# All 31 convolution taps on VectorE, a new order of a half, and the plan's durations taken from traces

## The chip, the cores and the metric

The kernel runs on 1 core of one Trainium2 chip. The metric is the device time of one execution in microseconds; lower is better. Before the change it is 1961.19 us, the median of 3 runs (1960.9 to 1964.42).

## The reference, cut to what matters

One layer of a hybrid decoder on 2048 prompt tokens and 8 single-token samples, width 1024, all in float32:

```
h    = rmsnorm(x)
proj = h @ w_in            # 48 chunks of 128 columns: c_a 8, c_b 8, c_z 8, s_x 4, s_z 4, g_c 8, g_s 8
u    = c_a * sigmoid(c_b)
v    = causal depthwise conv of u, 31 taps per channel, + bias
y_c  = (silu(layernorm(v)) * silu(c_z)) @ w_pc
y_s  = grouped complex-diagonal SSM of s_x, gelu, * sigmoid(. @ w_glu), * silu(s_z), @ w_ps
m    = sigmoid(g_c) * y_c + sigmoid(g_s) * y_s
x1   = x + rmsnorm(m @ w_out)
y    = x1 + rmsnorm(p @ w_ple) * sigmoid(x1 @ w_pg)
```

The outputs are y for both groups of tokens, the convolution's last inputs, and the SSM's states.

## The kernel before, in words

Channels lie on the 128 partitions, tokens along the free axis. The tokens are worked in two halves: half 0 is 1024 prompt tokens and the 8 samples (blocks of 344 columns, 258 for w_out and w_pg), half 1 the other 1024 (blocks of 512). Every float32 product is three passes over split operands: `hi` is a rounding to the fast matmul type, `lo` the rest, and each product sums hi·hi, hi·lo and lo·hi (`stages`, lines 289 to 291). A weight chunk of 512 KB is loaded from the SP queue, its `hi` cast on ScalarE, its `lo` subtracted on GpSimd (`w_split`), and `w_ahead` requests chunks two to three stages ahead in the fixed list `order`.

`half` runs the stages of a half on TensorE in this order: SX (SSM input, 4 chunks; in half 0 first for the first block, then for the other two), then CB and CA of each of 8 channel tiles, which give `u`; GC (8 chunks, stored to DRAM); SZ; w_glu; then GS two chunks at a time with w_ps; CZ (8 chunks); w_pc; w_out; w_pg. w_pc sums over all 8 tiles of `v`, so it can't begin until the layer norm has gone through all of them.

All else is laid beside these stages by a planner written out in Python (`Background`): tasks are generators that name an engine and a ready time; `pump` lets them emit instructions up to the planned time `bg.pe` of TensorE, by priority; `drain` emits a task's rest. Engines take instructions in the order emitted, so a wrong planned duration leaves a wrong order behind. The durations are `cV` (VectorE), `cS` (ScalarE), `cG` (GpSimd) and, per matmul, n/2400 + 0.003 us. A task that yields "P" puts small matmuls into TensorE's stream.

The tasks that matter here:

- `ssm_setup` (priority 6): small operations on VectorE for the SSM's parameters, then phases e^(i·k·theta) by doubling (`unit_length`, `cmul`: chains on 8 channels times 1, 2, 4 ... 64 elements), then four tables: VectorE makes `gt` from `gw`, TensorE transposes it (line 610) and multiplies it (620), GpSimd makes `cq`.
- `ssm_batch` (four a half): loads, matmuls (720), rotation by the phases and a scan on VectorE, matmuls (775, 778), and loads back.
- `conv_task` (priority 10): for each tile an opening multiplication and 30 multiply-adds of 1024 elements on VectorE, the sum `acc` in PSUM. If 8 units of SBUF are free, `conv_side` takes taps from the other end: ScalarE scales half a tile (`cq`, line 882), GpSimd adds it to `ca`; VectorE then adds `ca` (tile `u<-acc,ca`).
- `ln_task` (priority 4): sum over tiles, the mean by a matmul with a constant matrix, then per tile subtraction and square, a norm, and per tile scale, Silu, product with CZ's output and split into `vh`, `vl`.

SBUF is handed out in 38 units of 128 x 1096 elements; `room(k)` holds a task until k are free.

Of the kernel before, what the change touches and what calls it, by code (L numbers as in the profile page):

```python
# [13 lines left out]
P = 128  # L14
# [9 lines left out]
NUNIT = 38  # L24
UW = 1096


class Background:
# [105 lines left out]
def build(nc, tc, A, O):  # L134
# [23 lines left out]
    with ExitStack() as ctx:  # L158
# [60 lines left out]
        for h in range(2):  # L219
            if h == 0:  # L220
                order += [("w_ple", j) for j in range(2)]
            for _ in range(2 if h == 0 else 1):
                order += [("w_in", SX + b) for b in range(4)]
            for c in range(8):
                order += [("w_in", CB + c), ("w_in", CA + c)]
            order += [("w_in", GC + c) for c in range(8)]
            order += [("w_in", SZ + b) for b in range(4)]
            order += [("w_glu", j) for j in range(2)]
            for j in range(4):
                order += [("w_in", GS + 2 * j), ("w_in", GS + 2 * j + 1), ("w_ps", j)]  # L230
# [51 lines left out]
        def stages(key, todo):  # L282
            wt, k = take(key)
            for i, (m, rhs, evac, c0, n) in enumerate(todo):
# [9 lines left out]
                bg.pe += 3 * k * (n / 2400.0 + 0.003)  # L294
# [3 lines left out]
        def stage_pair(keys, rhs, blocks, evacs):  # L298
# [12 lines left out]
            bg.pe += 6 * len(rhs) * sum(n / 2400.0 + 0.003 for _, n in blocks)  # L311
# [36 lines left out]
        def mean_task(acc, blocks, bias, ready, k, split):  # L348
# [11 lines left out]
            yield "P", ready  # L360
# [32 lines left out]
        def norm_task(acc, blocks, ready, split=False):  # L393

            c = slice(blocks[0][0], blocks[-1][0] + blocks[-1][1])
            (tmp, y), r = yield from mean_task(acc, blocks, epsc, ready, 2, split)
# [14 lines left out]
        ud_d = [dram.tile([P, HT + NS], F32, name=f"ud{b}") for b in range(NB)]  # L411
        yd_d = [dram.tile([P, 8, 136], F32, name=f"yd{b}") for b in range(NB)]
# [18 lines left out]
        MAGIC = 12582912.0  # L431

# [15 lines left out]
        tables = {"done": 0}  # L448

        def ssm_setup():  # L450
# [20 lines left out]
            r0 = use("V", 5.6, 3.0)  # L471
# [8 lines left out]
            r0 = use("V", 1.6, r0)  # L480
# [25 lines left out]
            r0 = use("V", 4.0, r0)  # L506
# [19 lines left out]
            r0 = use("V", 6.0, r0)  # L526
# [16 lines left out]

            yield "V", r0
            tt(k1, mag, mag)
            tt(k1, k1, k1)
            tt(rho, k1, k1)
            ph = [[k1, k2], [k3, nre]]

            def unit_length(re, im, t):  # L550

                tt(t[0], re, re)
                tt(t[1], im, im)
                tt(t[0], t[0], t[1], ALU.add)
                ts(t[0], t[0], -0.5, 1.5)
                tt(re, re, t[0])
                tt(im, im, t[0])

            v2 = [wk[:, x * 16:x * 16 + 16] for x in range(2)]
            V.tensor_copy(out=ph[0][0], in_=cs)  # L560
            V.tensor_copy(out=ph[0][1], in_=sn)
            for x in range(3):
                unit_length(*ph[0], v2)
                cmul(*ph[1], *ph[0], *ph[0], *v2)
                ph.reverse()
            r0 = use("V", 6.5, r0)
            for x in range(2):
                yield from room(3)
                pu2 = [alloc(name="ph") for _ in range(3)]
                un = [t[:, 0:1024].rearrange("p (j k) -> p j k", k=P) for t in pu2[0:2]]  # L570
                w2 = [pu2[2][:, y * 512:(y + 1) * 512].rearrange("p (j k) -> p j k", j=8) for y in range(2)]
                s2 = [t[:, 0:8] for t in v2]
                yield "V", r0
                for r in range(2):
                    V.tensor_copy(out=un[r][:, :, 0], in_=ph[0][r][:, x * 8:x * 8 + 8])
                m = 1
                while m < P:
                    unit_length(un[0][:, :, m - 1], un[1][:, :, m - 1], s2)
                    base = [u_[:, :, m - 1:m].to_broadcast([P, 8, m]) for u_ in un]
                    cmul(un[0][:, :, m:2 * m], un[1][:, :, m:2 * m], un[0][:, :, 0:m], un[1][:, :, 0:m],  # L580
                         *base, w2[0][:, :, 0:m], w2[1][:, :, 0:m])
                    m *= 2
                    r0 = use("V", 2.0 + 6 * cV(4 * m), r0)
                    yield "V", r0
                for b in range(2 * x, 2 * x + 2):
                    for r in range(2):
                        dma(out=ph_d[b][:, r * 512:(r + 1) * 512],
                            in_=pu2[r][:, (b - 2 * x) * 512:(b - 2 * x + 1) * 512], after=r0)
                free(*pu2)
            r1 = max(r0, r1)  # L590
            for b in range(NB):
# [11 lines left out]
                r1 = use("V", 6 * cV(512), r1)  # L603
                we = alloc(name="we")
                wev = we[:, 0:1024].rearrange("p (j i r s) -> p j i r s", i=2, r=2, s=64)
                for r in range(2):
                    yield "P", r1
# [7 lines left out]
                yield "P", r1  # L615
# [7 lines left out]
                free(gt)  # L623
                yield "V", r3
# [13 lines left out]
                free(kdu, we)  # L638
                cq = alloc(name="cq")
# [18 lines left out]
                tables[b] = queue["data"] + 1.0  # L658
            free(bb, bcu, cbd, pu)
# [16 lines left out]
        def ssm_batch(h, b, sx, ysb, n, ready):  # L676
# [25 lines left out]
            phu = alloc(name="sph")  # L702
            rp = dma(out=phu[:, 0:1024], in_=ph_d[b], after=tables[b])
# [8 lines left out]
            for j0 in range(0, 4, 2):  # L712
                yield "P", r
# [16 lines left out]
            r = max(r1, rp)  # L730
# [16 lines left out]
            r = use("V", 2 * cV(1024) + 2 * cV(512), r)  # L747
# [6 lines left out]
            r = use("V", 8 * cV(256), r)  # L754
# [3 lines left out]
            r = use("V", 2 * cV(1024) + 2 * cV(512) + 0.2, r)  # L758
# [9 lines left out]
            for j0 in range(0, 4, 2):  # L768
                yield "P", r
# [51 lines left out]
        def conv_task(h, us, vs, seen):  # L821
            for c in range(NT):
                while us[c] is None:
                    yield None, bg.now + 0.5
# [9 lines left out]
                use("V", 0.4)  # L834
# [10 lines left out]
                use("V", 1.33)  # L845
                while left["lo"] <= left["hi"]:
# [6 lines left out]
                    r = use("V", 1.33)  # L853
# [34 lines left out]
        def sample_conv_task(seen):  # L888

            w = lambda c, k: cw[:, c, k:k + 1]  # L890
            for c in range(NT):
# [12 lines left out]
                use("V", 1.0, r)  # L904
# [23 lines left out]
        def embed(wait):  # L928

            for j in range(2):  # L930
                def ev_of(h, j=j):
# [3 lines left out]
                    def ev(m, o, c0, nn):  # L935
# [3 lines left out]
                        if c0 == 344:  # L939
                            V.tensor_copy(out=ts_[m][:, c0:c0 + nn], in_=o)  # L940
                            fore("V", cV(nn) + 0.06)
# [24 lines left out]
        def rms_task(todo):  # L966

            for nm, h in todo:
# [25 lines left out]
                r = yield from norm_task(acc, BLOCKS[h], ra, True)  # L994
# [85 lines left out]
        def half(h, hT, finish):  # L1080
# [16 lines left out]
            for k, part in enumerate(PARTS[h] if h == 0 else [[0, 1]]):  # L1097
                if finish:
                    finish(k)
                def ev_of(b):  # L1100
# [21 lines left out]
            us, vs = [None] * NT, [None] * NT  # L1122
            seen = [0, 0]
# [100 lines left out]
            def ln_sub(c, mean, acc, r):  # L1224
# [3 lines left out]
                if c:  # L1228
                    yield from room(1)
# [357 lines left out]
```

## Time and profile before

| what | value |
|---|---|
| runs | 1960.9, 1961.19, 1964.42 us; median 1961.19 |
| the profiled execution, in all | 1960.78 us |
| its span, first to last instruction | 1959.0 us |
| mean granted TensorE clock | 0.991 |
| busy share TensorE, VectorE, ScalarE, GpSimd | 98%, 73%, 39%, 40% |
| DMA | 243.63 MB, mean 124 GB/s |

The profile is one execution. "Busy" of TensorE joins overlapping matmuls, whose ends are modelled; a matmul's mean duration is therefore longer than the spacing between two of them. The granted clock is a share of full speed. Times in timelines count from the span's start.

### The profile page before, as it was taken

The page shows a single profiled execution, that of the slowest core. Times are in us where ns is not written, and L with a number is a line of the kernel's source. Part 1 is how long each engine was busy: PE and PEld are TensorE (multiplying, and loading weights), DVE is VectorE, ACT ScalarE, POOL GpSimd, SP SyncE. Part 2 cuts the span into 40 slices and gives each one's busy share as a digit, 9 for nine tenths or more (in the row PEclk, how much of TensorE's full clock was granted, in tenths as well). Part 3 has the DMA queues.
Part 4 walks back from the last instruction along what each step waited for, and adds up shares of the span by engine and source line. Part 5 has one row for each costly group of instructions (what it writes and reads, how often), then busy time and mean ns, then how long its engine had stood idle before and what let it go on. Part 6 is the DMA issues. An engine that isn't in the chain of part 4 may idle for free.

```text
span 1959.0 us, 27432 instructions
## 1 busy us (share of the span) xinstructions
PE 1915.9 (98%) x10772; PEld 1723.5 (88%) x10772; DVE 1438.4 (73%) x1703; ACT 769.3 (39%) x1301; POOL 784.2 (40%) x573
## 2 busy tenths in 40 slices
PE   8897999999999999999999999999999999999998
PEld 7897999999999999999997888888788888888876
DVE  6889997899899876446674579888499843341786
ACT  7424211228311364255533223455731353223542
POOL 1437523315422233234452222786743223224554
PEclk9898999999999999999999999999999999999999
DMA  8461334542122215334564563222112311432455
GB/s 316 152 209 56 106 133 142 181 141 71 57 89 80 99 43 194 120 95 144 193 207 162 183 204 119 65 65 97 66 43 76 99 65 44 161 108 86 140 193 172
DMA packets 103290, 243.63 MB, mean 124 GB/s; under 512 B 11752, under 2 KB 41576, under 8 KB 103144
## 3 DMA queue, kind: packets, MB, share of 16 engines
q1 hardware_dynamic: 102840, 241.68, 37.0%
q8 instruction: 84, 1.38, 0.3%
q14 instruction: 46, 0.38, 0.1%
q10 hardware_dynamic: 320, 0.20, 0.0%
HBM read 188.17 MB, written 54.62 MB: 124 GB/s over the span
## 4 chain that ended last, share of the span: by engine, by line
PE 84%; DVE 4%; issue 3%; POOL 2%; ACT 2%; DMA 1%; SPq 0%; ACTq 0%; POOLq 0%; DVEq 0%
PE bank L289 27%; PE bank L291 26%; PE bank L290 26%; PE bank L775 2%; POOL ca L332 1%; PE bank L778 1%; PE bank L720 1%; DVE sgp L332 1%; POOL wlo L332 1%; DVE o L183 1%; DMA raw<-in_w 1%; DVE spar L183 0%; DVE o L332 0%; PE bank L620 0%; DMA xn<-in_xT 0%
## 5 line engine op out<-in xcount | busy, mean ns | idle before, releaser
L332 POOL TENSOR_TENSOR wlo<-raw,whi 128x512 fp32r<-128x512 f32 x386 | 565.7, 1484 | 1072.2 <-ACT whi L252 1056.8
L289 PE MATMUL bank<-hh,whi 128*128 128x344 f32 (+1 forms) x1888 | 666.1, 353 | 0.9 <-ACT whi L252 0.9
L290 PE MATMUL bank<-hl,whi 128*128 128x344 f32 (+1 forms) x1888 | 661.4, 350 | 5.3 <-DVE hl L332 5.3
L291 PE MATMUL bank<-hh,wlo 128*128 128x344 f32 (+1 forms) x1888 | 659.8, 349 | 1.5 <-POOL wlo L332 1.5
L183 DVE SCALAR_TENSOR_TENSOR acc<-u,prm,acc 128x1024 f32<-128x1024 f32 x412 | 530.5, 1288 | 11.2
L289 PEld LDWEIGHTS bank<-hh,whi 128*128 128x128 f32 x1888 | 356.6, 189 | 37.5 <-ACT whi L252 1.5
L290 PEld LDWEIGHTS bank<-hl,whi 128*128 128x128 f32 x1888 | 357.1, 189 | 36.8 <-DVE hl L332 5.6
L291 PEld LDWEIGHTS bank<-hh,wlo 128*128 128x128 f32 x1888 | 357.4, 189 | 34.7 <-POOL wlo L332 2.5
L252 ACT CAST whi<-raw 128x512 fp32r<-128x512 f32 x388 | 223.9, 619 | 144.0 <-PE bank L290 68.7
L289 PE MATMUL bank<-mh,whi 128*128 128x258 f32 (+1 forms) x768 | 247.0, 322 | 2.2 <-ACT mh L339 1.7
L291 PE MATMUL bank<-mh,wlo 128*128 128x258 f32 (+1 forms) x768 | 246.6, 321 | 1.7 <-POOL wlo L332 1.6
L290 PE MATMUL bank<-ml,whi 128*128 128x258 f32 (+1 forms) x768 | 246.5, 321 | 0.4 <-DVE ml L332 0.3
L291 PEld LDWEIGHTS bank<-mh,wlo 128*128 128x128 f32 x768 | 145.6, 190 | 14.3 <-POOL wlo L332 3.0
L289 PEld LDWEIGHTS bank<-mh,whi 128*128 128x128 f32 x768 | 145.4, 189 | 14.2 <-ACT mh L339 1.9
L290 PEld LDWEIGHTS bank<-ml,whi 128*128 128x128 f32 x768 | 145.5, 189 | 12.5 <-DVE ml L332 1.0
L332 POOL TENSOR_TENSOR ca<-ca,cq 128x512 f32<-128x512 f32 x104 | 132.3, 1300 | 38.9 <-ACT cq L882 35.6
L290 PE MATMUL bank<-vl,whi 128*128 128x344 f32 (+1 forms) x320 | 111.9, 350 | 0.7 <-DVE vl L332 0.7
L289 PE MATMUL bank<-vh,whi 128*128 128x344 f32 (+1 forms) x320 | 112.0, 350 | 0.0
L291 PE MATMUL bank<-vh,wlo 128*128 128x344 f32 (+1 forms) x320 | 111.9, 350 | 0.0
L882 ACT ACTIVATE cq<-u,prm 128x512 f32<-128x512 f32 x104 | 73.4, 722 | 55.1 <-POOL ca L332 46.0
L332 DVE TENSOR_TENSOR oacc<-oacc,sq 128x258 f32<-128x258 f32 (+1 forms) x42 | 29.7, 721 | 70.2 <-ACT sq L1389 69.9
L177 DVE TENSOR_TENSOR gcl<-bank,gcl 128x344 f32<-128x344 f32 (+1 forms) x40 | 23.5, 587 | 65.4 <-PE bank L291 65.3
(213 smaller groups left out, 2452.0 us busy)
## 6 DMA issues: line engine op xcount, KB each, us to landing
raw<-in_w SPq DMA_DIRECT2D x194, 512.0 KB
cq<-cq SPq DMA_DIRECT2D x12, 512.0 KB
e<-e SPq DMA_DIRECT2D x8, 516.0 KB
rt<-e SPq DMA_DIRECT2D x8, 516.0 KB
gc<-gc SPq DMA_DIRECT2D x8, 516.0 KB
m<-gs SPq DMA_DIRECT2D x8, 516.0 KB
gcl<-gc SPq DMA_DIRECT2D x8, 516.0 KB
m2l<-m SPq DMA_DIRECT2D x8, 516.0 KB
```

Source lines behind the costliest of these rows:

```text
L177: V.tensor_tensor(out=out, in0=a, in1=b, op=op)
L183: V.scalar_tensor_tensor(out=out, in0=a, scalar=s, in1=b, op0=op0, op1=op1)
L252: S.copy(out=hi, in_=t[:, c])
L289: T.matmul(o, hi[:, w], rh[:, c0:c0 + n], start=kt == 0, stop=False)
L290: T.matmul(o, hi[:, w], rl[:, c0:c0 + n], start=False, stop=False)
L291: T.matmul(o, lo[:, w], rh[:, c0:c0 + n], start=False, stop=kt == k - 1)
L332: (V if e == "V" else GP).tensor_tensor(out=out, in0=a, in1=b, op=op)
L720: T.matmul(pvs[rr][half_[i], jj], we[:, g * P + rr * 64:g * P + rr * 64 + 64], U[:, g, 8:8 + ne], start=True, stop=True)
L775: T.matmul(pvs[i][:, jj], TW[:, :, 2 * j + i], U[:, 2 * j + i, o0:136], start=True, stop=False)
L778: T.matmul(pvs[i][:, jj], cq[half_[i], x * 512 + j * P:x * 512 + (j + 1) * P], X[half_[i], x, j, o0:136], start=False, stop=x == 1)
L882: S.activation(out=q[:, h], in_=u[:, k + x * 512:k + x * 512 + 512], func=AF.Identity, scale=w(k))
```

## The change

1. **Order of a half.** In half 0, CB and CA of two tiles (`EARLY`) come first, for the first block and then for the other two, in SX's place; SX follows once, for all blocks. Each later pair CB, CA (in half 1 each of the eight) is followed by two of the 16 gate chunks (GC, then GS); both gates go to DRAM. The rest of the gates come after, then SZ, w_glu, w_ps (its gates loaded back by `load_gs`), CZ, w_pc, w_out, w_pg.
2. **Taps.** `conv_side` is not started any more: all 31 taps on VectorE.
3. **Spilling.** After a tile of `v` is in the layer norm's sum, tiles 0 to 5 (`NSPILL`) are stored to `v_d` in DRAM. `back_task` is added when w_ps's stages are emitted, and loads them again; the norm's subtraction waits for it.
4. **Phases.** Instead of the doubling chains: angle times 1 to 128 on GpSimd, range reduction on VectorE, sine and cosine on ScalarE, double angle and length correction on GpSimd and VectorE, for 1024 elements at a time, in a task of its own (priority 6.1) that the tables don't wait for.
5. **Plan.** New durations; small matmuls of the SSM, the tables and most norms yield "Q", which is "P" with 9 us (`MARGIN`) added to the ready time; more `room` waits.

```
-        return "V" if v + n / 960.0 <= g + n / 478.0 + 0.3 else "G"
+        return "V" if v + n / 760.0 <= g + n / 440.0 + 0.4 else "G"
-    cV = lambda n: 0.08 + n / 960.0
+    cV = lambda n: 0.12 + n / 760.0
+    cVp = lambda n: 0.13 + n / 950.0
-    cS = lambda n: 0.13 + n / 1250.0
-    cG = lambda n: 0.16 + n / 478.0
+    cS = lambda n: 0.15 + n / 1100.0
+    cG = lambda n: 0.3 + n / 440.0
+    cPr = lambda n: 0.007 + n * 0.4375e-3
...
+                if e == "Q":
+                    e, r = "P", r + MARGIN
...
-            r0 = use("V", 5.6, 3.0)
+            r0 = use("V", 11.0, 3.0)
...
+            def phases(x, r):
...
+                r = ew("G", v3(a), kb, part(hi), ALU.mult, 1024, r)
+                r2 = ew("G", v3(cp), kb, part(lo), ALU.mult, 1024, r)
+                yield "V", r
+                ts(q, a, MAGIC, None, ALU.add)
+                stt(a, q, -MAGIC, a, ALU.add, ALU.subtract)
...
+                S.activation(out=sp, in_=a, func=AF.Sin, scale=PI)
+                S.activation(out=cp, in_=q, func=AF.Sin, scale=-PI, bias=hpi)
...
-                yield "P", r
+                yield "Q", r
...
-                if units.left() >= 8:
-                    left["hi"] -= 1
-                    a2 = alloc(name="ca")
-                    side = bg.add(conv_side(c, u, a2, left, bg.clock["V"] + 0.2), 9.5)
...
+                    if c < NSPILL and not lnt["back"]:
+                        yield None, r
+                        dma(out=v_d[h][c * P:(c + 1) * P, 0:n], in_=v, after=r)
+                        free(vs[c][0])
...
+            def back_task():
+                lnt["back"] = True
+                for c in list(lnt["out"]):
+                    yield from room(6)
+                    t = alloc(name="v")
+                    vs[c] = t, dma(out=t[:, PAD:PAD + n], in_=v_d[h][c * P:(c + 1) * P, 0:n])
...
+            for c in range(0 if h else EARLY, NT):
+                u_tile(c, blocks)
+                for _ in range(2):
+                    gate(gate_at)
+                    gate_at += 1
...
+            bg.add(back_task(), 3.8)
```

## Rows read from the trace of the kernel before

**Rows 1.** The page's first part: busy us, share, instructions of each engine.
```profile
PE 1915.9 (98%) x10772; PEld 1723.5 (88%) x10772; DVE 1438.4 (73%) x1703; ACT 769.3 (39%) x1301; POOL 784.2 (40%) x573
```

**Rows 2.** TensorE's waits, whole span: releaser, us in total, times, longest.
```profile
PE bank L610 <- issue: 14.1, 1, 14.1
...
PE bank L290 <- DVE hl L332: 5.3, 1, 5.3
```

**Rows 3.** Windows: length, busy us (instructions) of each engine, granted clock, DMA share, GB/s.
```profile
49.00:98.00 49.00, 41.96 (x224) 39.51 (x224) 42.55 (x101) 23.37 (x41) 21.74 (x30) 0.90 0.44 152
...
1029.00:1078.00 49.00, 45.79 (x214) 37.09 (x213) 23.69 (x22) 15.36 (x24) 13.87 (x10) 0.97 0.49 161
...
1470.00:1519.00 49.00, 49.00 (x214) 39.72 (x213) 45.97 (x40) 8.91 (x16) 16.47 (x12) 1.00 0.24 77
```

**Rows 4.** Timeline of TensorE at line 610: start, us, line, tiles, [idle before].
```profile
181.70 0.32 PE L290 MATMUL bank<-hl,whi 128*128 128x344 f32 x1
181.86 0.32 PE L291 MATMUL bank<-hh,wlo 128*128 128x344 f32 x1
196.23 1.09 PE L610 MATMUL bank<-ident,gt 128*128 128x128 f32 x4 [14.06 <-issue]
...
197.40 0.49 PE L290 MATMUL bank<-hl,whi 128*128 128x344 f32 x1
197.69 0.49 PE L291 MATMUL bank<-hh,wlo 128*128 128x344 f32 x1
```

**Rows 5.** Windows of 10 us at the stop, columns as in rows 3.
```profile
190.00:200.00 10.00, 3.77 (x15) 3.80 (x16) 9.69 (x18) 1.21 (x2) 1.28 (x1) 0.50 0.45 159
200.00:210.00 10.00, 10.00 (x67) 9.98 (x67) 9.75 (x10) 4.77 (x8) 5.25 (x5) 0.93 0.13 52
```

**Rows 6.** Timeline of VectorE ahead of the stop.
```profile
174.65 1.15 DVE L177 TENSOR_TENSOR spar<-spar 128x8 f32<-128x8 f32 x1
...
188.23 0.17 DVE L177 TENSOR_TENSOR spar<-spar 128x8 f32<-128x8 f32 x1
...
195.44 0.69 DVE L177 TENSOR_TENSOR gt<-gw 128x512 f32<-128x512 f32 x1
```

**Rows 7.** Timeline of GpSimd in the same stretch.
```profile
174.44 7.94 POOL L332 TENSOR_TENSOR ca<-ca,cq 128x512 f32<-128x512 f32 x6
```

**Rows 8.** Groups by line and form: busy us, mean ns, idle time before.
```profile
L183 DVE SCALAR_TENSOR_TENSOR acc<-u,prm,acc 128x1024 f32<-128x1024 f32 x412 | 530.5, 1288 | 11.2
...
L332 POOL TENSOR_TENSOR ca<-ca,cq 128x512 f32<-128x512 f32 x104 | 132.3, 1300 | 38.9 <-ACT cq L882 35.6 <-PE bank L291 3.4
...
L177 DVE TENSOR_TENSOR u<-acc,ca 128x1024 f32<-128x1024 f32 x6 | 7.3, 1224 | 31.9 <-POOL ca L332 31.8
```

**Rows 9.** Windows of tile ca alone: VectorE, ScalarE, GpSimd, then clock, DMA.
```profile
0.00:1040.00 1040.00, 1.22 (x1) 1.23 (x1) 33.49 (x26) 0.99 0.41 136
1040.00:1960.00 920.00, 6.12 (x5) 6.21 (x5) 98.79 (x78) 1.00 0.34 111
```

**Rows 10.** Window of tile ph alone: VectorE.
```profile
98.00:196.00 98.00, 55.85 (x144) 0.94 0.42 133
```

**Rows 11.** Windows up to the last tap of each half, columns as in rows 3.
```profile
98.00:667.00 569.00, 554.54 (x3602) 546.53 (x3601) 519.63 (x710) 174.30 (x320) 211.47 (x167) 0.99 0.35 115
1098.00:1534.00 436.00, 435.69 (x2030) 353.79 (x2029) 369.29 (x346) 180.43 (x275) 226.12 (x160) 1.00 0.30 98
```

**Rows 12.** Timeline of VectorE: the layer norm's stretch in both halves.
```profile
679.30 1.23 DVE L332 TENSOR_TENSOR u<-u,mean 128x1032 f32<-128x1032 f32 x1 [3.32 <-ACT mean L375]
...
754.46 1.23 DVE L332 TENSOR_TENSOR vl<-cz,vh 128x1032 fp32r<-128x1032 f32 x1 [1.12 <-ACT vh L339]
...
1543.21 1.23 DVE L332 TENSOR_TENSOR u<-u,mean 128x1024 f32<-128x1024 f32 x1 [5.52 <-ACT mean L375]
...
1594.27 5.10 DVE L332 TENSOR_TENSOR u<-u,acc 128x1024 f32<-128x1024 f32 x3
```

**Rows 13.** Tile vh: w_pc's weight loads, ns min/median/max, first and last start.
```profile
L289 PEld LDWEIGHTS bank<-vh,whi x320: 187/188/193, 751.3 to 1770.4; 128*128 128x128 f32 x160
```

More of the change, by code (lines that the diff above doesn't have):

```diff
@@ L24 @@
 NUNIT = 38
+NSPILL = 6
+MARGIN = 9.0
+EARLY = 2
 UW = 1096
@@ L310, in stage_pair @@
             w_ahead(wstate["use"], 0)
-            bg.pe += 6 * len(rhs) * sum(n / 2400.0 + 0.003 for _, n in blocks)
+            bg.pe += 6 * len(rhs) * sum(cPr(n) for _, n in blocks)
             bg.pump(pe=False)
@@ L346, in hilo, with mean_task @@
             return alloc(F32R, name=name + "h"), alloc(F32R, name=name + "l")
-        def mean_task(acc, blocks, bias, ready, k, split):
+        def mean_task(acc, blocks, bias, ready, k, split, late=False):
             yield from room(3 if split else k)
@@ L411, in build @@
         ud_d = [dram.tile([P, HT + NS], F32, name=f"ud{b}") for b in range(NB)]
+        v_d = [dram.tile([D, HT + NS], F32, name=f"v{h}") for h in range(2)]
         yd_d = [dram.tile([P, 8, 136], F32, name=f"yd{b}") for b in range(NB)]
@@ L446, in exp_dve @@
             tt(out, q, ki.bitcast(F32))
-        tables = {"done": 0}
+        tables = {"done": 0, "phases": 0}
         def ssm_setup():
@@ L505, in ssm_setup @@
             tt(fim, k1, k3)
-            r0 = use("V", 4.0, r0)
+            r0 = use("V", 7.0, r0)
+            yield "V", r0
+            tt(rho, mag, mag)
+            tt(rho, rho, rho)
+            tt(rho, rho, rho)
+            kk = pu[:, 944:1072]
+            yield "G", 0.0
+            GP.memset(kk[:, 0:1], 1.0)
+            m = 1
+            while m < P:
+                GP.tensor_scalar(out=kk[:, m:2 * m], in0=kk[:, 0:m], scalar1=float(m), scalar2=None, op0=ALU.add)
+                m *= 2
@@ L507, in ssm_setup, with phase_task @@
+            def phase_task(r):
+                for x in range(2):
+                    yield from phases(x, r)
+            bg.add(phase_task(r0), 6.1)
             yield "V", r0
@@ L658, in ssm_setup @@
                 tables[b] = queue["data"] + 1.0
+            while tables["phases"] < NB:
+                yield None, bg.now + 0.5
             free(bb, bcu, cbd, pu)
@@ L729, in ssm_batch @@
             free(we)
-            r = max(r1, rp)
+            while tables["phases"] < b + 1:
+                yield None, bg.now + 1.0
+            yield from room(3)
+            phu = alloc(name="sph")
+            r = max(r1, dma(out=phu[:, 0:1024], in_=ph_d[b], after=tables["ph", b // 2]))
+            yield from room(2)
             tmp, tm2 = alloc(name="stmp"), alloc(name="stmq")
@@ new lines, in half, with ln_sub @@
+            cz, vT = [None] * NT, [None] * NT
+            zr = [0.0] * NT
+            lnt = {"back": False, "out": []}
+            def back_task():
[4 more added lines that the diff above has]
+                    vs[c] = t, dma(out=t[:, PAD:PAD + n], in_=v_d[h][c * P:(c + 1) * P, 0:n])
+            def ln_sub(c, mean, acc, r):
+                r = max(r, vs[c][1])
+                yield "V", r
+                v = vs[c][0][:, PAD:PAD + n]
+                r = ew("V", v, v, mean[:, full], ALU.subtract, n, r)
+                if c:
+                    yield from room(1)
+                q = alloc(name="sq") if c else acc
+                yield "S", r
+                S.activation(out=q[:, full], in_=v, func=AF.Square)
+                r = use("S", cS(n), r)
+                if c:
+                    while not lnt["sub"][0][3]:
+                        yield None, bg.now + 0.5
+                    e = bg.pick(n, r)
+                    yield e, r
+                    r = ew(e, acc[:, full], acc[:, full], q[:, full], ALU.add, n, r)
+                    free(q)
+                lnt["r"] = max(lnt["r"], r)
@@ L1099, in half @@
+            ln = bg.add(ln_task(), 4)
+            conv = bg.add(conv_task(h, us, vs, seen), 10)
+            samp = bg.add(sample_conv_task(seen), 9) if h == 0 else None
+            if h == 0:
+                for k, part in enumerate(PARTS[h]):
                     finish(k)
+                    for c in range(EARLY):
+                        u_tile(c, [blocks[i] for i in part])
+            for part in [list(range(len(blocks)))]:
                 def ev_of(b):
@@ L1294, in half, with load_gs @@
-            ln = bg.add(ln_task(), 4)
+            gl = {}
+            def load_gs(j):
+                gl[j] = [unit("gs") for _ in range(2)]
+                for m, t in enumerate(gl[j]):
+                    dma(out=t[:, 0:n], in_=m2_d[h][(2 * j + m) * P:(2 * j + m + 1) * P, 0:n])
+            load_gs(0)
             for j in range(4):
-                gs = [unit("gs") for _ in range(2)]
-                for x in range(2):
-                    stage(("w_in", GS + 2 * j + x), hT, blocks, act_to(gs[x], AF.Sigmoid))
```

345 lines of the change are left out of this document (179 added, 166 removed).

## The prediction

> **What bounds the kernel now.** I read the page's first part first: TensorE is busy 1915.9 of 1959 us, every other engine at most 73% [rows 1]. So the end is set by TensorE's own stream, and a change that issues the same matmuls can only win what TensorE loses, or add to it. The steady rate shows that the matmuls themselves can't shrink: 344 columns start every 0.16 us [rows 4], 512 columns every 49.00/214 = 0.229 us [rows 3]. The idle time is 1959.0 - 1915.9 = 43.1 us. The waits of TensorE name one stop above all, 14.1 us at line 610; the next that the change touches is 5.3 us for `hl` of the first half [rows 2]. The windows put some loss in the first 98 us and around the change of halves, with the clock at 0.90 and 0.97 there [rows 3].
>
> The stop at line 610 is the transpose of `gt`, a table of the SSM that the plan placed in TensorE's stream among the matmuls of the big stages. TensorE reached it at 182.2 us; VectorE finished `gt` at about 196.1 [rows 4, 6]. The reason is on VectorE: the chain of phases ahead of `gt` works on 8 elements at a time, and such an instruction takes 0.17 us while GpSimd is quiet (at 188.23) but 1.15 us while GpSimd adds taps to `ca` (at 174.65; six of them run from 174.44 to 182.38) [rows 6, 7]. The plan priced neither.
>
> **The change part by part.** TensorE's work is the same: as many weight tiles, blocks and small SSM matmuls as before, in another order. What moves is what it waits for.
>
> 1. *The stop at line 610 goes.* The phase chain leaves VectorE (55.85 us of it between 98 and 196 us, counting only what touches `ph` [rows 10]), `gt` no longer stands behind it, GpSimd adds no taps, and the SSM's TensorE pieces are placed 9 us later than the planner thinks them ready ("Q"). Worth 14.06 us of idle time, and the slow restart: the granted clock is 0.50 from 190 to 200 us and 0.93 from 200 to 210 [rows 5], and matmuls of 344 columns start every 0.29 us instead of 0.16 at first [rows 4]. That is the lower of the two levels, 1.2 GHz, until about 200 + 0.07 x 10 x 2 = 201.4 us; from 196.2 to 201.4 half of 5.2 us is lost, 2.6. Together 16.7 us. Bounds: 0, if the stop only moves, and 16.7. I take 16.7, since cause and cover are both addressed. What is late next at this place is the same `gt` behind GpSimd: six table operations planned at 6 x (0.12 + 512/760) = 4.8 us. The new phases put 14 operations of 1024 elements on GpSimd, each about 2 x 1.3 = 2.6 us by the adds of 512 [rows 8]; if each of the six waits out one, they take 15.6 us, 10.8 over the plan, 1.8 more than the margin.
>
> 2. *All taps on VectorE.* GpSimd made 26 half-width adds in half 0 and 78 in half 1, which is 13 and 39 taps, with 1 and 5 opening taps on ScalarE and as many joining adds on VectorE [rows 9]. Half 0: VectorE gains 14 x 1.288 - 1.22 = 16.8 us; half 1: 44 x 1.288 - 6.1 = 50.6 us [rows 8]. Against it half 0 loses the 55.85 us, and gets eight phase operations of at most 1.288 us, 10.3. None of this is on TensorE's path as long as the layer norm's inputs are ready when CZ begins (point 4). GpSimd loses 132.3 us and gets 14 x 2.6 = 36; its other work is the weight split, which leaves it 60% idle [rows 1], so I cost both at nothing.
>
> 3. *Is the convolution in time?* Half 0: from 98 us to the end of the last tap at 667 VectorE was busy 519.6 of 569 us, 91% [rows 11]. Now 519.6 + 16.8 - 55.85 + 10.3 = 490.9 us; at 91% this takes 538 us and ends at 636 (at 100% at 589). CZ takes 8 x 72 x 0.157 = 90.4 us ahead of w_pc, which began at 751.3 [rows 13], so it began at 660.9 and now, 16.7 earlier, at 644. Half 1: 369.3 + 50.6 = 420 us from 1098 - 17 = 1081; 31.9 us of VectorE's idle time were waits for `ca` that go [rows 8], so its share is 369.3/404 = 91% and the end 1081 + 461 = 1542. CZ of half 1 begins at 1770.4 - 88.1 (the last weight load of w_pc less 8 x 48 x 0.229) - 88.1 - 16.7 = 1577.
>
> 4. *Layer norm now starts when CZ does, and must end with it.* Six of eight convolved tiles go out to DRAM and come back after w_ps. The loads are 0.52 MB each, 3.2 us at the 161 GB/s of the busiest row shown [rows 3]; VectorE takes about 2.5 us a tile, so all but the first 3 to 5 us lie beside the subtraction of the mean. The stretch from the first subtraction to the last `vl` was 679.3 to 755.7 = 76.4 us in half 0 [rows 12]. With 4 us of load and 9 us of margin ahead of the variance's matmul this is 89.4 us, against 90.4 of CZ. In half 1 subtraction to last scaling took 1543.2 to 1599.4 = 56.2 us; with eight products and splits of 2 x 1.23 us behind it 75.9, plus 13 = 88.9 against 88.1. So both just fit. The mean's own 15 us (split, margin, matmul) lie before CZ in half 1, and in half 0 end at 651, 7 us into CZ: there 76.4 + 9 from 651 ends at 736, w_pc is due at 751.3 - 16.7 = 734.6. Cost of this point: 0 to 5 us, I take 1, as the 76.4 contain 4 us of waits for CZ itself.
>
> 5. *The new waits.* The SP queue gets 8 more gate stores, 8 gate loads and 12 stores and loads of `v_d` a half. A store of `v_d` waits for the norm's sum, and behind it in that queue stand the next weight loads; w_ahead requests them two to three stages ahead, 22 to 34 us at 72 x 0.157 = 11.3 us a stage, so a store late by less costs nothing. The 28 x 0.52 = 14.5 MB a half more is some 90 us of transfer at 161 GB/s [rows 3], spread over 600 us: hidden.
>
> 6. *The start.* CB and CA of two tiles take SX's place, same matmuls. VectorE gets 6 evacuations of 344 elements, each below the 1.288 us of 1024 [rows 8], in the stretch where TensorE waited 5.3 us for `hl` [rows 2]. Bounds: 7.7 us lost, or up to 10.2 won (5.3, and 0.10 x 49 of clock [rows 3]) if the honest price of the SSM setup now keeps it from getting ahead of the last `hl`. I take 0.
>
> Sum: the profiled execution took 1960.8 us in all (span 1959.0), 0.4 below the median of 1961.2, so I work from it: 1960.8 - 16.7 + 1 = **1945 us**, by the first case's own uncertainty 1937 to 1952.
>
> **The rivals.**
>
> *A. The honest prices also win back the start and the change of halves.* Start 5.3 + 4.9; from 1029 to 1078 us 3.2 of idle time and 0.03 x 49 = 1.5 of clock [rows 3]. 1945 - 15 = 1930. For: those waits, too, stand behind VectorE work that the old plan priced low (`cV` for 1024 elements says 1.15 us, the subtractions took 1.23 or more [rows 12]). Against: no edit is aimed at them.
>
> *B. VectorE becomes the bound ahead of w_pc, and the kernel slower.* Every microsecond by which the last tap of half 0 passes 636 goes through the norm into a stop before w_pc. If VectorE runs at 86% (waits for the more closely planned evacuations, GpSimd's blocking), the taps end at 98 + 571 = 669, 33 us past 636, of which 1 to 3 are in the sum already: 1945 + 30 = 1975. It decides from 490.9/554 = 89% on: there the taps end at 652 and the gain of 16 is used up. For: the norm fills CZ to the microsecond in both halves. Against: in the stretch before, VectorE lost its time to waits that the new plan places later. The Trainium skill (Perfetto Trace Analysis, section "Optimizing Scalar/DVE Operations") would speak for B: work of a saturated VectorE is better moved to ScalarE or even GpSimd, though it adds that VectorE and GpSimd share a read port, so that the move may not help. That the old taps on GpSimd slowed VectorE nearly sevenfold on small operations (0.17 to 1.15 us) is the part that this trace shows.
>
> *C. The stop stays in another form.* `gt` waits behind the phase work on GpSimd (point 1: 10.8 us late against 9 of margin, on each of up to four tables): 1.8 us at each of four tables, 7, or, if the tables also queue behind the rest of the phases, up to most of the old stop: 1947 to 1960, say 1955. For: 0.17 against 1.15 us beside GpSimd [rows 6, 7]. Against: the table operations need not meet the phases at all. The Trainium skill (SBUF — State Buffer, section "Who interferes with whom") states it as a rule: a VectorE instruction with two SBUF inputs and a GpSimd instruction that reads SBUF block each other, whichever comes second for the whole of the first. By that rule this move of phases to GpSimd has its price on VectorE; the small operations of this trace agree with it, and what 1024-element operations do to a table operation no row here shows.
>
> **How the numbers follow.** A difference under 0.2% (3.9 us) can't be told from none. Forecast 1945: 0.50. A: 0.17. B: 0.20. C: 0.13, half of it within 0.2%. So faster 0.50 + 0.17 + 0.07 = 0.74, same 0.06, slower 0.20. For 8 in 10 the range goes to A with a little below, and into the first half of B: 1926 to 1970.
>
> **What would show it.** Right: TensorE's waits name line 610 no more, and the clock is full from 180 to 210 us; GpSimd's `ca` group is gone; VectorE has some 480 tap instructions of 1.29 us; the last `vl` falls within about 3 us of the first matmul of w_pc in both halves. B would show as a wait of TensorE for `vh` or `vl`, with VectorE at taps after 650 us. C as waits at the lines of the transposes or at 720 to 780 in the old numbering. A as no wait for `hl` and full clock from 60 to 90 us. I am wrong if a new wait above 5 us stands at a place not named here, most likely on a weight load behind a store.

## The result, and the profile after

The changed kernel takes 2011.22 us, the median of 4 runs (2009.71 to 2012.44), beside 1961.05 us for the kernel before on the same chip (4 runs, 1960.41 to 1964.42): ratio 1.0252, 95% interval 1.0234 to 1.027. It is 50 us slower, where 1945 was forecast and 1970 was the top of the range. The profiled span is 2007.9 us.

First the busy time of each engine in the kernel after; it answers [rows 1].

```profile
PE 1935.0 (96%) x10772; PEld 1732.8 (86%) x10772; DVE 1439.9 (72%) x1565; ACT 712.5 (35%) x1208; POOL 683.4 (34%) x491
```

TensorE has the same 10772 matmuls. VectorE is no busier than before (1439.9 against 1438.4 us). No other engine became the bound; TensorE lost time. Its waits in the kernel after, answering [rows 2]:

```profile
PE bank L300 <- ACT whi L263: 22.3, 5, 6.9
PE bank L300 <- ACT mh L350: 10.5, 2, 10.3
PE bank L302 <- POOL wlo L343: 6.8, 6, 3.6
PE bank L300 <- ACT vh L350: 4.5, 2, 4.2
...
PE bank L300 <- ACT ynh L350: 3.3, 2, 1.7
PE bank L301 <- DVE ynl L343: 3.1, 3, 2.0
```

The stop at the transpose is gone from this list, and the windows at its place are full (answer to [rows 5]):

```profile
190.00:200.00 10.00, 10.00 (x82) 8.98 (x80) 9.79 (x9) 9.76 (x15) 6.91 (x5) 1.00 0.18 52
200.00:210.00 10.00, 10.00 (x69) 10.00 (x69) 9.71 (x12) 2.85 (x9) 5.21 (x5) 1.00 0.67 214
```

In its place stand waits for `whi` and `mh` (the stages w_out and w_pg), `wlo` (the last weight chunk of SZ above all), `ynh` and `ynl` (w_ps) and `vh` (w_pc). The longest wait for `whi`, 6.9 us, is no new one: it stands ahead of the very first matmul, as in the kernel before, so 15.4 of the 22.3 us lie elsewhere. From the waits of the kernel before:

```profile
PE bank L289 <- ACT whi L252: 8.3, 3, 6.9
```

The windows show where TensorE lost its time:

```profile
560.00:620.00 60.00, 52.28 (x304) 50.18 (x303) 51.86 (x56) 22.10 (x37) 24.32 (x13) 0.94 0.30 99
740.00:780.00 40.00, 33.41 (x196) 31.96 (x195) 25.32 (x30) 16.98 (x23) 7.25 (x5) 0.91 0.43 146
900.00:940.00 40.00, 32.74 (x252) 32.17 (x251) 24.32 (x35) 20.17 (x44) 14.09 (x10) 0.87 0.39 128
...
1940.00:1960.00 20.00, 9.10 (x35) 6.29 (x34) 12.17 (x16) 5.00 (x9) 7.01 (x4) 0.74 0.59 195
```

The last column but two is the granted clock, 0.74 to 0.94 here, and a list of waits leaves out what the lower clock after each stop costs. So I also took, from TensorE's timeline, each gap from one large matmul's start to the next start, less the steady gap (0.157 us for 344 columns, 0.230 for 512, 0.1205 for 258) and less the small matmuls between, and summed the excess by stage. This table, in us, is my working from the timelines of the kernels named in it. Its totals differ by 50.4 us between before and after, the spans by 48.9. The column w_ps takes in the SZ stages just ahead: of the 18.4 us, 11.0 are waits for w_ps's own input and 7.4 waits of SZ for its weights' split.

```
                           start  SSM tables   w_ps   ahead of   w_out,  change of   rest  total
                           <105   and scan            w_pc       w_pg    halves
before                     15.3    20.1         0.0     1.0        8.3      6.4       2.1   53.2
after                      15.5     2.8        18.4     9.5       43.5     11.5       2.4  103.6
e1 old scaling price       14.9     2.8        19.2     9.6       15.9      2.2       2.3   66.8
e2 all old durations       10.9     9.0        19.4    34.5        9.1      5.9       2.0   90.9
e3 gates late              14.8     3.9         0       9.6       41.6     11.4       2.3   83.5
e4 before + new durations  16.1    25.2         0       1.0       44.3     11.5       9.4  107.5
e5 before + scaling price  15.4    20.1         0.0     1.0       45.4      2.3       2.5   86.7
e6 = e1 and e3             15.4     3.7         0      10.1       15.7      1.4       1.9   48.1
e7 = e6, no norm margin    15.3     3.7         0       1.0       16.3      2.2       1.8   40.3
e8 before + all taps       15.0     3.6         0.2    26.0        8.5      5.4       3.1   61.9
```

The change won 17.3 us at the tables and lost 67.7: 18.4 around w_ps, 8.5 ahead of w_pc, 35.2 in w_out and w_pg, 5.1 at the change of halves, 0.5 in the rest.

### The profile page after: what moved, and what is told of

The parts are those of the page before. It is cut to its first block, busy times and chain, and to the rows that moved or that the text cites. A ratio compares the mean times of both kernels' runs of the same rounds, so it can differ in the third digit from the quotient of the medians.

```text
span 2007.9 us, 27201 instructions
## 1 busy us (share of the span) xinstructions
PE 1935.0 (96%) x10772; PEld 1732.8 (86%) x10772; DVE 1439.9 (72%) x1565; ACT 712.5 (35%) x1208; POOL 683.4 (34%) x491
## 4 chain that ended last, share of the span: by engine, by line
PE 86%; issue 4%; DVE 4%; ACT 3%; POOL 2%; DMA 1%; SPq 0%; POOLq 0%; DVEq 0%; ACTq 0%
PE bank L300 27%; PE bank L302 27%; PE bank L301 27%; POOL wlo L343 2%; PE bank L827 2%; PE bank L830 1%; PE bank L767 1%; DVE hl L343 1%; ACT z L1328 0%; DVE xn L190 0%; DVE xT L190 0%; DVE acc L190 0%; DVE spar L190 0%; DMA raw<-in_w 0%; PE bank L665 0%
## 5 line engine op out<-in xcount | busy, mean ns | idle before, releaser
L343 POOL TENSOR_TENSOR wlo<-raw,whi 128x512 fp32r<-128x512 f32 x386 | 560.0, 1468 | 1219.5 <-ACT whi L263 1210.0
L190 DVE SCALAR_TENSOR_TENSOR acc<-u,prm,acc 128x1024 f32<-128x1024 f32 x464 | 597.6, 1288 | 12.8
L302 PEld LDWEIGHTS bank<-mh,wlo 128*128 128x128 f32 x768 | 148.0, 193 | 15.5 <-POOL wlo L343 4.1
L334 ACT ACTIVATE gc<-bank 128x344 f32<-128x344 f32 (+1 forms) x80 | 41.0, 514 | 262.7 <-PE bank L302 262.7
L184 DVE TENSOR_TENSOR u<-bank,sg 128x344 f32<-128x344 f32 (+1 forms) x40 | 23.0, 580 | 79.1 <-PE bank L302 78.2
```

Of the source, the lines that this page charges most:

```text
L184: V.tensor_tensor(out=out, in0=a, in1=b, op=op)
L190: V.scalar_tensor_tensor(out=out, in0=a, scalar=s, in1=b, op0=op0, op1=op1)
L302: T.matmul(o, lo[:, w], rh[:, c0:c0 + n], start=False, stop=kt == k - 1)
L334: S.activation(out=t[:, c0:c0 + n], in_=o, func=func)
L343: (V if e == "V" else GP).tensor_tensor(out=out, in0=a, in1=b, op=op)
```

## The experiments

Time of the kernel before beside them: 1961.2 us (e1 to e4), 1961.05 (e5 to e8), 1961.2 (e9 to e11), 1960.1 (e12, e13); medians throughout.

**e1: the price of one operation.** Each tile of w_out's output is scaled by the row norm (`o<-o,prm,oacc`, 32 times), beside the stages w_out and w_pg. The change set its planned duration to 1.42 us for 512 columns. e1 is the kernel after with the general price `cV` (0.79 us) there:

```
-                r = max(use("V", 0.2 + m / 420.0, r), rx)
+                r = max(use("V", cV(m), r), rx)
```

> The changed kernel with one planned duration put back: the scaling of w_out's output (516 or 512 elements) at cV(m) = 0.8 us instead of 0.2 + m/420 = 1.43. Theory P (VectorE overpriced): in the changed kernel this scaling took 0.75 us, so the plan's VectorE clock runs ahead of the real one at the end of a half, tasks are emitted too late or in a lump ahead of evacuations and weight casts, and TensorE loses 24 us more than before around w_out and w_pg (lost time 15.1 against 4.3 us at 920 to 1000 us, 28 against 3.2 at 1860 to 1970). If this one price does it: 1980 to 1990 us. If it takes all the new prices of VectorE: 2000 to 2011. Theory O (the order of stages, gates gone from between w_glu and w_ps, norm squeezed into CZ): 2011 unchanged. Theory T (taps, VectorE saturated): 2011.

1976.6 us, ratio to before 1.0082 (1.0067 to 1.0097): 34.6 us come back by one number, more than the 21 to 31 expected. What the price does is seen on ScalarE's queue in w_out. The kernel after:

```profile
917.94 0.62 ACT L350 CAST mh<-o 128x516 fp32r<-128x516 f32 x1 [2.19 <-DVE o L343]
921.23 0.63 ACT L350 CAST mh<-o 128x516 fp32r<-128x516 f32 x1 [2.66 <-DVE o L343]
...
928.48 0.62 ACT L350 CAST mh<-o 128x516 fp32r<-128x516 f32 x1 [1.37 <-DVE o L343]
929.01 0.37 ACT L332 COPY o<-bank 128x258 f32<-128x258 f32 x1
929.27 1.14 ACT L263 CAST whi<-raw 128x512 fp32r<-128x512 f32 x2
```

and TensorE there:

```profile
929.94 0.58 PE L300 MATMUL bank<-mh,whi 128*128 128x258 f32 x1 [6.42 <-ACT whi L263]
```

The same queue in e1:

```profile
916.98 0.62 ACT L350 CAST mh<-o 128x516 fp32r<-128x516 f32 x1 [1.75 <-DVE o L343]
...
917.83 0.36 ACT L332 COPY o<-bank 128x258 f32<-128x258 f32 x1
918.08 1.14 ACT L263 CAST whi<-raw 128x512 fp32r<-128x512 f32 x2
...
924.83 1.23 ACT L350 CAST mh<-o 128x516 fp32r<-128x516 f32 x2 [1.13 <-DVE o L343]
925.97 0.37 ACT L332 COPY o<-bank 128x258 f32<-128x258 f32 x1
926.23 1.15 ACT L263 CAST whi<-raw 128x512 fp32r<-128x512 f32 x2
```

With the higher price the plan's VectorE clock runs ahead, and by the code a `drain` then issues six tiles' casts in a row (the three at 922.01, 924.50 and 926.49 us are left out above). Each waits for VectorE; the weight's cast and the copy of TensorE's bank wait behind them. In e1 they alternate.

**e2: the old durations, new order.** The seven changed rules put back; the single numbers that the change set anew inside tasks (such as 11.0 for 5.6 in `ssm_setup`) stay.

> The changed kernel with all planned durations of before (cV, cS, cG, the matmuls', the choice between VectorE and GpSimd, the scaling), but its order, taps, spilling, phases and margin. Theory P: the losses around w_out and w_pg go, 35 us: 1972 to 1982, perhaps some back because the matmuls are priced 7% too short again. Theory O: losses at w_ps (12 us in half 0, 6 in half 1) and ahead of w_pc (8 us) stay, total 2005 to 2015. Theory T: 2011 or worse, as VectorE is priced too low for 31 taps.

1998.5 us, 1.0192 (1.0177 to 1.0208), between the expectations. The loss in w_out and w_pg is gone (9.1), but 34.5 us stand ahead of w_pc: the last tap of half 0 ends at 683.0 us, where the kernel after has 651.9. So in the new order the other new durations are worth some 22 us (1998.5 against e1's 1976.6), and the scaling's alone is harmful. In the old order they are not (e4).

**e3: cover between w_glu and w_ps.** The kernel after with the last four gate chunks of each half between w_glu and w_ps (stage order and weight order alike):

```
-                order += [("w_in", CB + c), ("w_in", CA + c)] + gates[:2]
-                gates = gates[2:]
-            order += gates
+                order += [("w_in", CB + c), ("w_in", CA + c)]
+                if len(gates) > 4:
+                    order += gates[:2]
+                    gates = gates[2:]
             order += [("w_in", SZ + b) for b in range(4)]
             order += [("w_glu", j) for j in range(2)]
+            order += gates
...
```

> The changed kernel with the last four gate chunks computed after w_glu, ahead of w_ps, in both halves. Theory O: w_ps began 0 us after w_glu and waited for the split of its own input (ynh, ynl) and for weights; with 45 us of gates between, the 6.6 us at 600 and 4.4 at 1560 us go, the 5.7 at 560 stay: 1997 to 2003. Theory P and T: 2008 to 2014.

1991.9 us, 1.0158 (1.0143 to 1.0173): 19.3 us less than after, as the 18.4 of the table said, and below the 1997 to 2003 expected, because the wait near 560 us, which was to stay, went too. What it removes, on TensorE in the kernel after:

```profile
567.46 0.65 PE L302 MATMUL bank<-hh,wlo 128*128 128x344 f32 x1 [3.63 <-POOL wlo L343]
...
604.46 0.42 PE L300 MATMUL bank<-ynh,whi 128*128 128x344 f32 x1 [1.58 <-ACT ynh L350]
...
606.84 0.42 PE L301 MATMUL bank<-ynl,whi 128*128 128x344 f32 x1 [1.96 <-DVE ynl L343]
```

w_ps takes `yn`, which w_glu's last result ends; between them is a sigmoid, a product and a split of four tiles. The old order laid a pair of GS chunks there; the new one laid nothing. The first row is another matter: there the last SZ chunk waits for its weight's split on GpSimd. Why the later gates end that wait too isn't shown. The window of e3 is full:

```profile
560.00:620.00 60.00, 60.00 (x381) 59.83 (x380) 50.62 (x55) 19.41 (x30) 14.47 (x12) 1.00 0.51 181
```

**e4: the new durations in the old order,** with the old taps (and the `room` waits that keep SBUF from running out).

> The kernel before with the new planned durations alone (VectorE, ScalarE, GpSimd, matmuls, choice, the scaling), and units asked for before they are taken. Theory P: it loses at w_out and w_pg like the changed kernel: 1961 + 25 to 35 = 1986 to 1996, less what the stop at the table's transpose loses by better prices. My forecast's view (honest durations only help): 1944 to 1958, the stop smaller. Theories O and T: within 1955 to 1965.

2016.9 us, 1.0287 (1.027 to 1.0304), above every expectation. The durations alone make the old kernel as slow as the whole change, and the stop at the transpose stays as two waits for `gt`, 10.7 us together (25.2 in its column). The scaling's price is 32 of the 56 us (e5); most of the other 24 stands in the columns of the tables, the change of halves and the rest.

**e5: the scaling's price alone in the kernel before.** The line of e1, the other way.

> The kernel before, with one line changed: the price of the scaling by g_post, 0.2 + m/420 in place of 0.08 + m/960 (1.42 us for 0.61 us at 512 columns). Theory P (this price alone sends the plan's VectorE clock ahead of the work at the output projection and the gate projection): 1990 us (1961.2 + 25 to 35), with the losses of the TensorE in 880-980 and 1860-1960. Rival (the price hurts only beside the new order, or only beside the other new durations): 1957 to 1966 us. Gain of the order alone aside, the stop at the transpose near 190 us stays in both.

1993.0 us, 1.0167 (1.0152 to 1.0182): 32 us by one planned number, no instruction changed. TensorE's waits in e5, to be read against [rows 2]:

```profile
PE bank L289 <- ACT whi L252: 21.2, 4, 7.1
PE bank L610 <- issue: 14.1, 1, 14.1
PE bank L289 <- ACT mh L339: 12.7, 4, 5.0
```

Was the price wrong, then? The scaling's group in the kernel before:

```profile
L183 DVE SCALAR_TENSOR_TENSOR o<-o,prm,oacc 128x512 f32<-128x512 f32 x16 | 21.9, 1393 | 0.0
```

and in e5:

```profile
L183 DVE SCALAR_TENSOR_TENSOR o<-o,prm,oacc 128x512 f32<-128x512 f32 x16 | 14.6, 935 | 0.0
```

The price of 1.42 us is close to the mean in the trace of before, 1.39. Put into the plan, it lumps the scalings while GpSimd's weight split waits for the very cast that is late (its rows stand in the last section); beside an idle GpSimd they take less. The honest number makes its own trace untrue, and the kernel slower.

**e6: e1 and e3 together.**

> The kernel after, with the last four gate chunks of each half between w_glu and w_ps, and the old price of the scaling. Theory P+O (the two losses stand apart and add): 1976.6 - 19.3 = 1957 us, between 1953 and 1961; TensorE's losses at 560-600, 900-940 and 1860-1970 gone, those ahead of w_pc (740: 7 to 9 us) and at the change of halves left. Rival (each moves the waits of the other): 1965 to 1977 us, with a new loss above 5 us.

1958.3 us, 0.9988 (0.9979 to 0.9997). The two effects add: 2011.2 - 34.6 - 19.3 = 1957.3.

**e7: e6 without the layer norm's margin.** Its two sums yield "P" and no longer "Q":

```
-                (mean,), r = yield from mean_task(acc, blocks, None, r, 1, True, True)
+                (mean,), r = yield from mean_task(acc, blocks, None, r, 1, True, False)
...
-                r = yield from norm_task(acc, blocks, lnt["r"], True, True)
+                r = yield from norm_task(acc, blocks, lnt["r"], True, False)
```

> As e6, and the layer norm's two TensorE sums without the 9 us that the plan adds to their due time. Theory M (the margin makes the layer norm late ahead of w_pc in half 0): e6 less 5 to 8 us, near 1950 us, w_pc's wait on vh gone. Rival T (the taps on VectorE make it late, since the last tap comes at 652 us): the loss at 740 stays, or comes back as a stop of TensorE at the sums themselves, 5 us or more: within 2 us of e6.

1946.6 us, 0.993 (0.9914 to 0.9947), 11.7 under e6, more than the 5 to 8 expected. The layer norm of half 0 in the kernel after, answering [rows 12]:

```profile
650.59 1.27 DVE L190 SCALAR_TENSOR_TENSOR u<-u,prm,acc 128x1024 f32<-128x1024 f32 x1
...
652.40 1.23 DVE L343 TENSOR_TENSOR acc<-acc,u 128x1032 f32<-128x1032 f32 x1
...
655.19 1.22 DVE L343 TENSOR_TENSOR nl<-acc,nh 128x1032 fp32r<-128x1032 f32 x1
671.40 3.52 DVE L343 TENSOR_TENSOR v<-v,mean 128x1032 f32<-128x1032 f32 x3 [14.98 <-ACT mean L386]
...
718.74 1.23 DVE L184 TENSOR_TENSOR acc<-acc,mean 128x1032 f32<-128x1032 f32 x1 [20.60 <-ACT acc L396]
...
757.42 1.23 DVE L343 TENSOR_TENSOR vl<-cz,vh 128x1032 fp32r<-128x1032 f32 x1 [1.12 <-ACT vh L350]
```

and in e7:

```profile
644.57 2.27 DVE L345 TENSOR_TENSOR acc<-acc,u 128x1032 f32<-128x1032 f32 x1
...
654.45 7.09 DVE L345 TENSOR_TENSOR v<-v,mean 128x1032 f32<-128x1032 f32 x4 [5.25 <-DMA v<-v]
...
687.68 1.23 DVE L184 TENSOR_TENSOR acc<-acc,mean 128x1032 f32<-128x1032 f32 x1 [8.33 <-ACT acc L398]
...
739.11 1.23 DVE L345 TENSOR_TENSOR vl<-cz,vh 128x1032 fp32r<-128x1032 f32 x1 [1.12 <-ACT vh L352]
```

The waits at the two sums fall from 14.98 and 20.60 to 5.25 and 8.33 us (the 5.25 is ended by the loading of `v`, no longer by the mean), and the last `vl` comes 18 us earlier.

**e8: the taps alone.** The kernel before with `if units.left() >= 8` made false, so all 31 taps on VectorE (and the `room` waits of e4).

> The kernel before with all 31 taps on VectorE (no tap on ScalarE and GpSimd), old order and old prices. Theory P+O (taps cost nothing): 1955 to 1965 us. Rival T (the taps are the slow part: VectorE is late for the convolution, the layer norm ends after 757 us): 1975 us or more, with the added loss of TensorE ahead of w_pc.

1969.0 us, 1.0046 (1.0031 to 1.0061), between the two expectations, and both are half right. The stop at the transpose goes (20.1 to 3.6) once GpSimd adds no taps, without any new phase code. But 26 us appear ahead of w_pc:

```profile
740.00:760.00 20.00, 8.90 (x21) 5.51 (x21) 18.68 (x18) 12.63 (x12) 0.00 (x0) 0.50 0.09 36
```

with TensorE waiting for the layer norm's result:

```profile
PE bank L289 <- ACT vh L339: 14.6, 3, 6.0
```

That is rival B as it was described, in the old order: VectorE busy 18.68 of 20 us and late. The new order alone doesn't cure it: e2 has the new order with the old durations, its last tap of half 0 ends at 683.0 us, beside 688.3 here, and it loses 34.5 us ahead of w_pc. The kernel after, with both, ends it at 651.9.

**e9: taps back on ScalarE and GpSimd, in e7.**

> As e7, and some taps back on ScalarE with GpSimd's sum beside (the helper is still in the file), as in the kernel before. Theory (in the new order the taps cost nothing on VectorE, since the convolution has room): within 1942 and 1951 us of e7's 1946.6. Rival T (VectorE is late by the taps): faster, below 1942 us. Rival S (GpSimd's sums hold up VectorE's small work): slower, above 1951 us, by waits on POOL wlo or on vh ahead of w_pc.

1952.5 us, 0.9956 (0.9941 to 0.9971): 5.8 above e7, just past the border of rival S. The waits that it named don't show; a new one does:

```profile
PE bank L302 <- ACT cq L936: 3.6, 1, 3.6
```

TensorE's bank waits for ScalarE, which is scaling a tap's half tile (`cq`). By the working of the table, the gaps from 1134 to 1156 us, with this stop in them, hold 12.9 us of excess, and the same place in e7 7.0. So all taps on VectorE gain some 6 us here, and they are this one stop in half 1 rather than a price of each tap.

**e10: e8 with the new durations** (but the old scaling price).

> As e8 (kernel before, all taps on VectorE), with the new durations but the old price of the scaling. If the order is what makes the taps late in e8 (VectorE has 123 taps of 1.29 us between 450 and 760 us there, 92 in the kernel after): the 26 us ahead of w_pc stay, 1965 us or more. Rival A (honest durations put each tap in time, whatever the order): below 1955 us, w_pc's waits under 5 us.

2035.2 us, 1.0377 (1.0362 to 1.0393). Neither theory held: w_pc's wait for `vh` fell to 4.8 us, below the 5 that the rival named, and the time rose by 66 us over e8. A stop stands at the SSM's output matmuls:

```profile
PE bank L784 <- issue: 49.8, 1, 49.8
```

Its releaser isn't named in the trace. The first matmuls of `ssm_batch`'s output stand at 441.5 us, those with the scan's states at 492.6; the states' last rotation on VectorE, among the taps, starts at 491.8. By that, the new durations put the scan late in the old order. They don't put the taps in time: the last tap of half 0 ends at 736.0 us, 48 later than in e8, and w_pc waits less because TensorE itself comes to it at 809.0, not at 742.0.

**e11: the margin alone, in the kernel after.**

> The kernel after, only without the 9 us added to the due time of the layer norm's two sums. Theory M: 2011.2 less 6 to 12 us, so 1999 to 2005 us (e7 against e6 was 11.7 less). Rival (that gain is there only with the gates after w_glu, which make room for the first sum): 2007 to 2015 us.

2003.5 us, 1.0218 (1.0201 to 1.0235): 7.7 less, as expected; the column ahead of w_pc falls from 9.5 to 1.0.

**e12: the path of the scaling's price.** The kernel after, price kept, with the cast of the next free weight issued before the evacuation that drains the plan:

```
+                if (key[0] in ("w_out", "w_pg") and i == len(todo) - 1
+                        and wstate["use"] < wstate["split"] < wstate["dma"]):
+                    w_split(wstate["split"])
+                    wstate["split"] += 1
                 bg.pe += 3 * k * cPr(n)
```

> The kernel after with its price of the scaling, and the casts of the weight after next issued ahead of the waiting work at each chunk of w_out and w_pg (ahead of the evacuation that drains the plan). Theory Q (the price costs time because the plan then issues the row scalings' six casts in a lump on ScalarE's queue, and the weight's cast stands behind them): TensorE's waits on whi (22.3 us in 5) fall below 8 us, and the time to 1988 to 1998 us. Rival R (the lump itself is late: TensorE then waits on mh, ml or a bank for as long): 2004 to 2014 us.

1999.2 us, 1.0202 (1.0185 to 1.0219), 12 less than after and between the two. TensorE's waits:

```profile
PE bank L300 <- ACT mh L354: 14.5, 5, 8.3
PE bank L300 <- ACT whi L263: 13.1, 5, 6.4
```

The waits for `whi`, less the one ahead of the first matmul, fall from 15.4 to 6.7 us; those for `mh` grow from 10.5 to 14.5. By the working of the table, 7.6 us come back at the change of halves and only 3.4 of the 35 lost in w_out and w_pg. So the weight's cast behind the lump is the smaller part there; most of the loss stays with the lump, as rival R said. How it divides between late `mh` and banks copied late isn't settled.

**e13: the same edit in e7.**

> e7 with the same edit. Theory Q: its one wait on whi (7.3 us near 1880 us) goes, 1938 to 1943 us. Rival R: another wait takes its place, 1944 to 1951 us.

1951.0 us, 0.9955 (0.9941 to 0.997), slower than e7 by 4.4, at the top of rival R's range. Theory Q had no wait to remove here: the 7.3 us for `whi` in e7 stand ahead of the first matmul, not near 1880 us. By the working of the table, e13 gains 1.7 us in w_out and w_pg and loses 5.7 at the change of halves. e7 stays the fastest, 0.7% under the kernel before.

## Why the prediction was wrong, point by point

**1. The stop at line 610: right.** Forecast 16.7 us, measured 17.3 in the table's column. e8 adds that the taps' move off GpSimd alone does it, and e4 that the new durations don't. Rival C (the stop in another form) did not come.

**2. Taps at nothing: right for the new order with the new durations.** e9 puts them at 6 us gained. In the old order with the old durations they cost 8 (e8), which the prediction had as B's mechanism and tied to neither.

**3. The convolution in time: too early by 16 us.** The last tap of half 0 was forecast to end at 636 and ends at 651.9 (the first of the rows under e7). VectorE was busy 508.6 of the 554 us up to there:

```profile
98.00:652.00 554.00, 546.28 (x3537) 536.38 (x3536) 508.61 (x541) 182.76 (x320) 223.19 (x167) 0.99 0.44 145
```

That is 92%, as assumed, but 17.7 us more work than the 490.9 summed. The sum took the SSM's work on VectorE at its old size; the 32 scans and the 16 operations next to them (`sc<-stmp,stmq`) took 37.2 us in this stretch, against 26.8 in the stretch of [rows 11]. Half 1 ended at 1597, not 1542, partly since TensorE's stops had moved everything back; there it cost nothing.

**4. The layer norm: mechanism right, size wrong.** It was taken at 1 us of 0 to 5, and is 8.5 (e7, e11). The prediction counted 4 us of load and 9 of margin, and saw that the norm fills CZ to the microsecond. By its own steps the last `vl` was to end 1.8 us after w_pc is due; it ended 11.5 after w_pc's first matmul (758.7 and 747.2 us). The mean came at 671.4, not 651, and w_pc at 747.2, not 734.6, since TensorE itself had stopped around w_ps. Of the 7.8 us between them the taps made 3.3, and the mean's sum 4.5 (19.5 us after the last tap, where 15 were counted); the stretch from there to the last `vl` took 87.3 us, not 85.4. In it the wait for the variance was 9.14 us before,

```profile
714.36 1.23 DVE L177 TENSOR_TENSOR acc<-acc,mean 128x1032 f32<-128x1032 f32 x1 [9.14 <-ACT acc L385]
```

and 20.60 after. This is rival B's place, but not its price. e11 leaves the last tap at 650.4, still 14 us past the forecast, drops the margin alone, and the column falls to 1.0; e6 has its last tap at 642.7, keeps the margin, and loses 10.1. So the margin made the cost.

**5. New waits on the SP queue: right.** TensorE's list names no DMA, so no weight load is seen to be late. The "new wait above 5 us at a place not named" did come, on a weight's cast behind other casts instead of a load behind a store.

**6. The start: right,** 15.3 and 15.5.

**The step that failed is one that the sum didn't have.** It stopped at six parts and put at nothing, without a reason, two things: the plan's new durations themselves, and the dependencies that the new stage order puts next to each other. Rival A took honest durations as something that could only gain. They lost 32 us in the old kernel by one number (e5) and 35 in the new (e1), because a planned duration doesn't describe the work, it decides the order of three queues. And the order `w_glu, w_ps` stood in the diff: w_ps needs what w_glu has just made, the old order had two chunks of 11.3 us between them, and no line of the prediction asked what covers it now; 11.0 us by the table, and 18.4 with the waits of SZ that go with it (e3). With these two and the margin undone, e7 takes 1946.6, next to the forecast of 1945, though not by its terms alone: 16.4 us won at the tables and 4.2 at the change of halves, 8.0 lost in w_out and w_pg.

Those 8.0 us go with the new durations that e7 keeps, not with the order or the taps: e2, in the new order with the old durations, has 9.1 us in w_out and w_pg, about as before, and in the old order e10 has, by the same working, 7 us more there than e8. Which of the durations it is stays open. The spilling and the new phases were not tried alone.

## What to carry to other kernels

A planner's duration is a control, not a measurement: when one is changed, ask which queue gets a lump and what stands behind it, and try each number alone. When stages are put in a new order, write down for each what made its input and how long ago; where the producer is the stage just ahead, the chain between them is bare. A margin added so that TensorE never waits is paid by whoever needs the result, and twice where two sums follow each other.

## What the runs showed of the hardware

The same instruction has two durations in one queue, by what GpSimd does. In the kernel after, VectorE:

```profile
913.19 1.79 DVE L190 SCALAR_TENSOR_TENSOR o<-o,prm,oacc 128x516 f32<-128x516 f32 x1
...
917.83 0.74 DVE L190 SCALAR_TENSOR_TENSOR o<-o,prm,oacc 128x516 f32<-128x516 f32 x1
```

and GpSimd, which has nothing between 916.1 and 929.97:

```profile
913.03 3.11 POOL L343 TENSOR_TENSOR wlo<-raw,whi 128x512 fp32r<-128x512 f32 x2 [2.60 <-ACT whi L263]
929.97 1.56 POOL L343 TENSOR_TENSOR wlo<-raw,whi 128x512 fp32r<-128x512 f32 x1 [13.83 <-ACT whi L263]
```

The rule of the Trainium skill (SBUF — State Buffer, section "Who interferes with whom") that the prediction quoted says this: the one that comes second waits for the first. The trace agrees that it is held up: 1.05 us more, within one GpSimd subtraction of 1.56, though less than the 1.40 us that this subtraction still had to run. The taps, whose running sum is in PSUM, are not touched, though 198 of these 464 ran beside a GpSimd instruction (min/median/max in e7):

```profile
L190 DVE SCALAR_TENSOR_TENSOR acc<-u,prm,acc x464: 1253/1290/1292, 106.6 to 1550.1; 128x1024 f32<-128x1024 f32 x155
```

So a single planned price for the scaling can't be right, whatever its value, while the taps' can.
